# A hybrid decoder layer on one core: moving operands of TensorE laid out as two runs, even columns and odd columns

## The chip, the cores and the metric

The kernel runs on one core of one Trainium2 chip. The metric is the device time of one execution in microseconds: 2041.44 us is the median of three runs before the change (2040.09 to 2043.89). Engines are named as in the profile: PE (TensorE, with PEld for its weight loads), DVE (VectorE), ACT (ScalarE), POOL (GpSimd) and SP (SyncE, which issues the DMAs).

## The reference

One layer for 256 tokens of 2048 features, all in fp32: two SwiGLU blocks with 5632 hidden features around a token mixer, each behind an RMSNorm that a condition vector scales and shifts, and a last RMSNorm.

```python
def swiglu(h, wg, wu, wd):
    return (jax.nn.silu(h @ wg) * (h @ wu)) @ wd
...
    cond = jax.nn.silu(c)
    for l in range(DEPTH):
        mod = cond @ ada_w[l] + ada_b[l]
        sh1, sc1, gt1, sh2, sc2, gt2, sh3, sc3, gt3 = jnp.split(mod, N_MOD, axis=-1)
        h = ada_in(x, norm_g[l, 0], sh1, sc1)
        x = x + MACARON_W * gt1[:, None, :] * swiglu(h, ffn_w_gate[l, 0], ffn_w_up[l, 0], ffn_w_down[l, 0])
        h = ada_in(x, norm_g[l, 1], sh2, sc2)
        x = x + gt2[:, None, :] * hybrid_mixer(h, w_in[l], w_out[l], fox_f_bias[l], fox_out_norm[l],
                                               gdn_conv[l], gdn_A_log[l], gdn_dt_bias[l], gdn_out_norm[l])
        h = ada_in(x, norm_g[l, 2], sh3, sc3)
        x = x + MACARON_W * gt3[:, None, :] * swiglu(h, ffn_w_gate[l, 1], ffn_w_up[l, 1], ffn_w_down[l, 1])
    return rmsnorm(x, final_norm).astype(x.dtype)
```

`ada_in` is `rmsnorm(x, g) * (1 + scale) + shift`. The mixer projects `h` once, runs eight heads of forgetting attention (fox) and eight heads of a gated delta rule (gdn) side by side, and projects their outputs back with `w_out`.

## The kernel before

The activations stand with features on the partitions: a tile of 128 features by 256 tokens. All weights are 5392 tiles of 128x128, stored in the order in which the kernel uses them, eight to a block of 512 KB. `Stream.next` hands out the next tile. For a new block it starts the DMA into `wraw` (line 96), casts the block on ACT to a rounded fp32 format, `whi` (line 98), and subtracts on DVE to get the rest, `wlo` (line 110). Activations are split in the same way into a high part HI and a low part LO. A product is then made of three single-pass matmuls: high by high, high by low and low by high. Between blocks, at a pace set by the table `RATE`, `ada_col` fetches and reduces a row of the conditioning matrix (`mod`, line 230).

TensorE holds a weight tile and lets the activation pass as the moving operand, 256 columns of HI, 256 of LO, or 512 of both in one matmul:

- `hs` holds the normed input of a stage, 16 feature tiles `k` of LO, HI and a pad of 64 columns, of which two hold the split shift in the third norm (`Early`). Readers are `three` (first SwiGLU's first 28 hidden tiles, three matmuls of 256 columns, lines 518 to 520, outputs `pgu`), `mm_h` (the other gate and up tiles, one matmul of 512 columns and one of 256, lines 432 and 433, outputs `pg` and `pu`), `Early.products` (lines 376 to 378: the first three tiles of the second SwiGLU, with the two shift columns) and the mixer's `project` (lines 706 to 708, outputs `pp`).
- `hid` tiles hold the gated hidden features, `oh` tiles the heads' outputs, each as [HI, LO] of 256 columns. `mm` reads them (lines 436 and 437, outputs `pd` for the down projections and `po` for the output projection).
- In `project_rows` (lines 719 to 721, outputs `pv`) the roles change: a slice of `hs` is held, and four weight tiles of a block pass as 512 moving columns.

These operands are written by `modulate_one` and `Early.y` (`hs`), `split` (`hid`) and `out_split` (`oh`): ACT writes HI, then DVE writes LO.

The program's order is that of the code, with small reorderings by the scheduling layer; the mixer's heads are generators advanced by a clock that counts matmuls (`tick`, `start`, `finish`). The stages are: start and first SwiGLU up to about 770 us, the mixer to about 1290 us, with the output projection as its last 100 us, then the second SwiGLU and the last norm.

Of the kernel before, what the change touches and what calls it, by code (L numbers as in the profile page):

```python
# [28 lines left out]
WB = 8  # L29
# [13 lines left out]
HS = 2 * 256 + 64  # L43
# [26 lines left out]
N_COL = _n  # L70


class Stream:
# [27 lines left out]
    def next(self, mat, k, n, width=1):  # L101
# [13 lines left out]
        for d in range(width):  # L115
            self.order.append((mat, k, n + d))
        o = (i % WB) * P
        return self.h[:, o : o + width * P], self.l[:, o : o + width * P]
# [3 lines left out]
def layer_kernel(ctx: ExitStack, tc: tile.TileContext, xrow, c, adaw, cols, cst, w, out, order, dbg=None):  # L122
# [191 lines left out]
    hs = hsf[:, : KD * HS].rearrange("p (k i) -> p k i", k=KD)  # L314
    LO, HI, HIS, ALL = slice(0, T), slice(T, 2 * T), slice(T, 2 * T + 2), slice(0, 2 * T)

    def modulate_one(j, g1, sh, r):

        t = pt("ht")
        V.scalar_tensor_tensor(t, x[:, j], g1, r, ALU.mult, ALU.mult)  # L320
        if j % 2:
            A.activation(t, t, AF.Identity, bias=sh)
            A.copy(hs[:, j, HI], t)  # L323
            return V.tensor_tensor(hs[:, j, LO], t, hs[:, j, HI].bitcast(F32), ALU.subtract)
        else:
            with tc.issue_after(W.cast) if W.first else nullcontext():
                A.activation(hs[:, j, HI], t, AF.Identity, bias=sh)
            return V.scalar_tensor_tensor(hs[:, j, LO], t, sh, hs[:, j, HI].bitcast(F32), ALU.add, ALU.subtract)
# [8 lines left out]
    def modulate(which, m_sh, m_sc):  # L337
# [4 lines left out]
            j, g1[:, j : j + 1], mod[:, m_sh * KD + j : m_sh * KD + j + 1], r)  # L342

    class Early:
# [6 lines left out]
        def y(self, j):  # L351
# [3 lines left out]
            if j == 0:  # L355
                sh = mod[:, self.m_sh * KD : (self.m_sh + 1) * KD]
                A.copy(hs[:, :, 2 * T], sh)
                V.tensor_sub(hs[:, :, 2 * T + 1], sh, hs[:, :, 2 * T].bitcast(F32))
            g = gains(self.which, self.m_sc, j, 1)
            A.activation(hs[:, j, HI], x[:, j], AF.Copy, scale=g)  # L360
            V.scalar_tensor_tensor(hs[:, j, LO], x[:, j], g, hs[:, j, HI].bitcast(F32), ALU.mult, ALU.subtract)
# [13 lines left out]
        def products(self, ps, wt, k):  # L375
            PE.matmul(ps[:, : T + 2], wt[0], hs[:, k, HIS], start=(k == 0), stop=False)
            PE.matmul(ps[:, :T], wt[0], hs[:, k, LO], start=False, stop=False)
            PE.matmul(ps[:, : T + 2], wt[1], hs[:, k, HIS], start=False, stop=(k == KD - 1))
# [52 lines left out]
    def mm_h(ps, wt, k):  # L431
        PE.matmul(ps, wt[0], hs[:, k, ALL], start=(k == 0), stop=False)  # L432
        PE.matmul(ps[:, T:], wt[1], hs[:, k, HI], start=False, stop=(k == KD - 1))  # L433
# [908 lines left out]
```

## Time and profile before

| | |
|---|---|
| median of the runs | 2041.44 us (2040.09, 2041.44, 2043.89) |
| span of the profiled execution | 2038.5 us, granted TensorE clock 0.993 on average; the page gives no other time of this execution |
| PE, PEld | 98% and 89% busy |
| DVE, ACT, POOL | 77%, 50% and 3% busy |
| HBM read | 512.89 MB, 254 GB/s over the span |

The span runs from the first to the last instruction of one execution; a timed run also has what lies around it. [...]

### The profile page before, as it was taken

The page shows a single profiled execution, that of the slowest core. Times are in us where ns is not written, and L with a number is a line of the kernel's source. Part 1 is how long each engine was busy: PE and PEld are TensorE (multiplying, and loading weights), DVE is VectorE, ACT ScalarE, POOL GpSimd, SP SyncE. Part 2 cuts the span into 40 slices and gives each one's busy share as a digit, 9 for nine tenths or more (in the row PEclk, how much of TensorE's full clock was granted, in tenths as well). Part 3 has the DMA queues.
Part 4 walks back from the last instruction along what each step waited for, and adds up shares of the span by engine and source line. Part 5 has one row for each costly group of instructions (what it writes and reads, how often), then busy time and mean ns, then how long its engine had stood idle before and what let it go on. Part 6 is the DMA issues. An engine that isn't in the chain of part 4 may idle for free.

```text
span 2038.5 us, 33631 instructions
## 1 busy us (share of the span) xinstructions
PE 1998.6 (98%) x13058; PEld 1818.5 (89%) x13059; DVE 1566.0 (77%) x2424; ACT 1021.5 (50%) x1607; POOL 64.7 (3%) x60
## 2 busy tenths in 40 slices
PE   8999999999999999999999999999999999999997
PEld 6999999888888888889989988988888888888886
DVE  6898978889888998779878889976666555555555
ACT  6544544333444446666655655654444344444442
POOL 0000000000000120000000002000000000000012
PEclk9999999999999999999999999999999999999998
DMA  9999867999889885676666668667776655555553
GB/s 338 350 327 327 288 212 262 372 344 368 334 338 331 336 306 187 232 243 236 219 242 221 222 229 304 234 223 241 252 231 218 193 188 189 193 187 191 192 187 113
DMA packets 129489, 519.56 MB, mean 255 GB/s; under 512 B 18217, under 2 KB 21545, under 8 KB 111153
## 3 DMA queue, kind: packets, MB, share of 16 engines
q1 hardware_dynamic: 129330, 517.42, 72.1%
q8 instruction: 102, 1.67, 0.3%
q14 instruction: 57, 0.47, 0.1%
HBM read 512.89 MB, written 4.47 MB: 254 GB/s over the span
## 4 chain that ended last, share of the span: by engine, by line
PE 86%; DVE 6%; ACT 2%; DMA 2%; issue 2%; SPq 0%; DVEq 0%; ACTq 0%
PE pd L436 15%; PE pu L432 10%; PE pg L432 10%; PE pd L437 8%; PE pu L433 5%; PE pg L433 5%; PE pgu L520 5%; PE pgu L518 5%; PE pgu L519 5%; PE pp L706 3%; PE pp L708 3%; PE pp L707 3%; DVE wlo L110 2%; DMA wraw<-in_w_dram 2%; PE po L436 2%
## 5 line engine op out<-in xcount | busy, mean ns | idle before, releaser
L110 DVE TENSOR_TENSOR wlo<-wraw,whi 128x1024 fp32r<-128x1024 f32 x674 | 822.5, 1228 | 307.2 <-ACT whi L98 304.3
L98 ACT CAST whi<-wraw 128x1024 fp32r<-128x1024 f32 x674 | 702.0, 1049 | 630.2 <-issue 153.4
L436 PE MATMUL pd<-hid,whi 128*128 128x512 f32 x1408 | 488.5, 390 | 0.0
L437 PE MATMUL pd<-hid,wlo 128*128 128x256 f32 x1408 | 397.3, 282 | 1.0 <-DVE wlo L110 0.8
L230 DVE CUSTOM_DVE_ANT_0 adat<-adat,cs,colt 128x2048 f32<-128x2048 f32 x140 | 329.3, 2352 | 35.9 <-DMA adat<-in_ada_dram 35.7
L432 PE MATMUL pg<-hs,whi 128*128 128x512 f32 x912 | 318.9, 390 | 0.5 <-DVE shc L384 0.4
L432 PE MATMUL pu<-hs,whi 128*128 128x512 f32 x912 | 318.7, 390 | 0.0
L436 PEld LDWEIGHTS pd<-hid,whi 128*128 128x128 f32 x1408 | 264.1, 188 | 55.0
L437 PEld LDWEIGHTS pd<-hid,wlo 128*128 128x128 f32 x1408 | 266.1, 189 | 3.0 <-DVE wlo L110 2.7
L433 PE MATMUL pg<-hs,wlo 128*128 128x256 f32 x912 | 257.2, 282 | 0.0
L433 PE MATMUL pu<-hs,wlo 128*128 128x256 f32 x912 | 257.1, 282 | 0.0
L518 PE MATMUL pgu<-hs,whi 128*128 128x256 f32 x896 | 249.0, 281 | 6.8 <-ACT hs L323 5.7
L520 PE MATMUL pgu<-hs,wlo 128*128 128x256 f32 x896 | 248.0, 281 | 1.9 <-DVE wlo L110 1.8
L519 PE MATMUL pgu<-hs,whi 128*128 128x256 f32 x896 | 249.8, 281 | 0.0
L432 PEld LDWEIGHTS pg<-hs,whi 128*128 128x128 f32 x912 | 171.1, 188 | 36.7 <-ACT shc L383 0.5
L432 PEld LDWEIGHTS pu<-hs,whi 128*128 128x128 f32 x912 | 171.1, 188 | 35.7
L706 PE MATMUL pp<-hs,whi 128*128 128x256 f32 x656 | 189.7, 290 | 2.4 <-ACT whi L98 1.2
L708 PE MATMUL pp<-hs,wlo 128*128 128x256 f32 x656 | 186.2, 285 | 0.3 <-DVE wlo L110 0.3
L707 PE MATMUL pp<-hs,whi 128*128 128x256 f32 x656 | 185.7, 283 | 0.0
L518 PEld LDWEIGHTS pgu<-hs,whi 128*128 128x128 f32 x896 | 168.7, 189 | 7.7 <-ACT hs L323 6.1
L433 PEld LDWEIGHTS pu<-hs,wlo 128*128 128x128 f32 x912 | 172.3, 189 | 0.2
L433 PEld LDWEIGHTS pg<-hs,wlo 128*128 128x128 f32 x912 | 172.4, 189 | 0.0
(334 smaller groups left out, 2572.0 us busy)
## 6 DMA issues: line engine op xcount, KB each, us to landing
wraw<-in_w_dram SPq DMA_DIRECT2D x674, 512.0 KB, 4.4
adat<-in_ada_dram SPq DMA_DIRECT2D x140, 1024.0 KB, 7.1
xr<-in_xr_dram SPq DMA_DIRECT2D x4, 512.0 KB, 6.3
adaf<-in_ada_dram SPq DMA_DIRECT2D x4, 512.0 KB, 8.7
adaf<-in_ada_dram SPq DMA_DIRECT2D x2, 1024.0 KB, 12.5
xd<-x SPq DMA_DIRECT2D x4, 512.0 KB, 8.3
rw<-rowd SPq DMA_DIRECT2D x16, 128.0 KB, 6.7
x<-xd SPq DMA_DIRECT2D x4, 512.0 KB, 8.8
```

Source lines behind the costliest of these rows:

```text
L98: self.cast = self.nc.scalar.copy(self.h, r).ins
L110: nc.vector.tensor_tensor(self.l, r, self.h.bitcast(F32), ALU.subtract)
L230: V.tensor_tensor_reduce(t, t, cs, 1.0, L("adab", q, 1), ALU.mult, ALU.add, mod[:, q : q + 1])
L432: PE.matmul(ps, wt[0], hs[:, k, ALL], start=(k == 0), stop=False)
L433: PE.matmul(ps[:, T:], wt[1], hs[:, k, HI], start=False, stop=(k == KD - 1))
L436: PE.matmul(ps, wt[0], act.rearrange("p a t -> p (a t)"), start=first, stop=False)
L437: PE.matmul(ps[:, :T], wt[1], act[:, 0], start=False, stop=last)
L518: PE.matmul(o, wh, hs[:, k, HI], start=first and s == 0, stop=False, skip_group_check=skip)
L519: PE.matmul(o, wh, hs[:, k, LO], start=False, stop=False, skip_group_check=skip)
L520: PE.matmul(o, wl, hs[:, k, HI], start=False, stop=last, skip_group_check=skip)
L706: PE.matmul(pp[i][:, :T], wh, hs[:, k, HI], start=(k == 0), stop=False)
L708: PE.matmul(pp[i][:, :T], wl, hs[:, k, HI], start=False, stop=(k == KD - 1))
```

## The change

The moving operands named above, except those of `project`, are stored as two runs. Column 2b lies at place b of the first run and column 2b+1 at place b of the second. TensorE then reads first place 0 of both runs, then place 1 of both, and so on, so that the columns arrive in their old order: the access pattern's innermost step is from run to run, and the matmuls' outputs are unchanged. In `hs` a run is 128 columns and 16 of pad (576 bytes from run to run), the two shift columns take one place in the pad of each HI run. In `hid` and `oh` the runs are 128 columns (512 bytes apart). For the row projections the columns of four weight tiles are packed so by the host, as runs of 256 (1024 bytes apart). ACT and DVE write HI and LO through the same pattern. In the mixer's norm `hs` is written plainly (`weave=False`), because `project_rows` holds slices of it; `plain` is that view.

```diff
...
 HIDX = 3
 MORE = True
 
-HS = 2 * 256 + 64
+HA = 128 + 16
+HS = 4 * HA
 PAD = {"hs": 16, "w": 56, "hid": 16, "more": 56}
 
 BACK = (4, 6, 9)
...
 N_COL = _n
 
 
+def woven(ap):
+
+    return ap.rearrange("p (a b) -> p b a", a=2)
+
+
+def pairs(ap):
+
+    return ap.rearrange("p (b a) -> p b a", a=2)
+
+
 class Stream:
 
 
...
                 self.owed -= 1.0
                 self.side()
         for d in range(width):
-            self.order.append((mat, k, n + d))
+            self.order.append((mat, k, n, width, d))
         o = (i % WB) * P
-        return self.h[:, o : o + width * P], self.l[:, o : o + width * P]
+        h, l = self.h[:, o : o + width * P], self.l[:, o : o + width * P]
+        return (h, l) if width == 1 else (woven(h), woven(l))
 
 
 @with_exitstack
...
 
 
     hsf = keep.tile([P, KD * HS + PAD["w"]], F32R, name="hs")
-    hs = hsf[:, : KD * HS].rearrange("p (k i) -> p k i", k=KD)
-    LO, HI, HIS, ALL = slice(0, T), slice(T, 2 * T), slice(T, 2 * T + 2), slice(0, 2 * T)
-
-    def modulate_one(j, g1, sh, r):
+    hs = hsf[:, : KD * HS].rearrange("p (k q a b) -> p k q a b", k=KD, q=2, a=2)
+    LO, HI = 0, 1
+
+    plain = hsf[:, : KD * HS].rearrange("p (k i) -> p k i", k=KD)[:, :, : 2 * T].rearrange("p k (q t) -> p k q t", q=2)
+
+    def part(k, q, extra=0):
+        return hs[:, k, q, :, : P + extra].rearrange("p a b -> p b a")
+
+    def modulate_one(j, g1, sh, r, weave=True):
 
         t = pt("ht")
+        hl, hh, tt = (part(j, LO), part(j, HI), pairs(t)) if weave else (plain[:, j, LO], plain[:, j, HI], t)
         V.scalar_tensor_tensor(t, x[:, j], g1, r, ALU.mult, ALU.mult)
         if j % 2:
             A.activation(t, t, AF.Identity, bias=sh)
-            A.copy(hs[:, j, HI], t)
-            return V.tensor_tensor(hs[:, j, LO], t, hs[:, j, HI].bitcast(F32), ALU.subtract)
+            A.copy(hh, tt)
+            return V.tensor_tensor(hl, tt, hh.bitcast(F32), ALU.subtract)
         else:
             with tc.issue_after(W.cast) if W.first else nullcontext():
-                A.activation(hs[:, j, HI], t, AF.Identity, bias=sh)
-            return V.scalar_tensor_tensor(hs[:, j, LO], t, sh, hs[:, j, HI].bitcast(F32), ALU.add, ALU.subtract)
+                A.activation(hh, tt, AF.Identity, bias=sh)
+            return V.scalar_tensor_tensor(hl, tt, sh, hh.bitcast(F32), ALU.add, ALU.subtract)
 
     def gains(which, m_sc, j, n):
 
...
         g1 = gains(which, m_sc, 0, KD)
         r = norm_row(norm_sums())
         hq["next"], hq["one"] = 0, lambda j: modulate_one(
-            j, g1[:, j : j + 1], mod[:, m_sh * KD + j : m_sh * KD + j + 1], r)
+            j, g1[:, j : j + 1], mod[:, m_sh * KD + j : m_sh * KD + j + 1], r, False)
 
     class Early:
 
...
             ada_need(self.m_sh, KD - 1)
             if j == 0:
                 sh = mod[:, self.m_sh * KD : (self.m_sh + 1) * KD]
-                A.copy(hs[:, :, 2 * T], sh)
-                V.tensor_sub(hs[:, :, 2 * T + 1], sh, hs[:, :, 2 * T].bitcast(F32))
+                A.copy(hs[:, :, HI, 0, P], sh)
+                V.tensor_sub(hs[:, :, HI, 1, P], sh, hs[:, :, HI, 0, P].bitcast(F32))
             g = gains(self.which, self.m_sc, j, 1)
-            A.activation(hs[:, j, HI], x[:, j], AF.Copy, scale=g)
-            V.scalar_tensor_tensor(hs[:, j, LO], x[:, j], g, hs[:, j, HI].bitcast(F32), ALU.mult, ALU.subtract)
+            A.activation(part(j, HI), pairs(x[:, j]), AF.Copy, scale=g)
+            V.scalar_tensor_tensor(part(j, LO), pairs(x[:, j]), g, part(j, HI).bitcast(F32), ALU.mult, ALU.subtract)
 
         def step(self, k):
 
...
                 h_upto(min(k, k - 4 + max(0, k - 10)))
 
         def products(self, ps, wt, k):
-            PE.matmul(ps[:, : T + 2], wt[0], hs[:, k, HIS], start=(k == 0), stop=False)
-            PE.matmul(ps[:, :T], wt[0], hs[:, k, LO], start=False, stop=False)
-            PE.matmul(ps[:, : T + 2], wt[1], hs[:, k, HIS], start=False, stop=(k == KD - 1))
+            PE.matmul(ps[:, : T + 2], wt[0], part(k, HI, 1), start=(k == 0), stop=False)
+            PE.matmul(ps[:, :T], wt[0], part(k, LO), start=False, stop=False)
+            PE.matmul(ps[:, : T + 2], wt[1], part(k, HI, 1), start=False, stop=(k == KD - 1))
 
         def scaled(self, dst, ps):
 
...
         chains[kind].append((h, chain))
 
     def mm_h(ps, wt, k):
-        PE.matmul(ps, wt[0], hs[:, k, ALL], start=(k == 0), stop=False)
-        PE.matmul(ps[:, T:], wt[1], hs[:, k, HI], start=False, stop=(k == KD - 1))
+        both = hs[:, k, :, :, :P].rearrange("p q a b -> p q b a")
+        PE.matmul(ps, wt[0], both, start=(k == 0), stop=False)
+        PE.matmul(ps[:, T:], wt[1], part(k, HI), start=False, stop=(k == KD - 1))
 
     def mm(ps, wt, act, first, last):
-        PE.matmul(ps, wt[0], act.rearrange("p a t -> p (a t)"), start=first, stop=False)
-        PE.matmul(ps[:, :T], wt[1], act[:, 0], start=False, stop=last)
+        PE.matmul(ps, wt[0], act.rearrange("p q (a b) -> p q b a", a=2), start=first, stop=False)
+        PE.matmul(ps[:, :T], wt[1], woven(act[:, 0]), start=False, stop=last)
 
     def merge(dst, ps, scale=None):
 
...
             V.scalar_tensor_tensor(dst, ps[:, :T], scale, t, ALU.mult, ALU.add)
 
     def split(dst, src):
-        A.copy(dst[:, 0], src)
-        V.tensor_sub(dst[:, 1], src, dst[:, 0].bitcast(F32))
+        A.copy(woven(dst[:, 0]), pairs(src))
+        V.tensor_sub(woven(dst[:, 1]), pairs(src), woven(dst[:, 0]).bitcast(F32))
 
     def residual(ps, j, m_gt, half):
         ada_need(m_gt, j)
...
             wh, wl = W.next(("gu"[s], 0), k, f)
             first, last = k == k0, k == k1 - 1
             skip = s == 1
-            PE.matmul(o, wh, hs[:, k, HI], start=first and s == 0, stop=False, skip_group_check=skip)
-            PE.matmul(o, wh, hs[:, k, LO], start=False, stop=False, skip_group_check=skip)
-            PE.matmul(o, wl, hs[:, k, HI], start=False, stop=last, skip_group_check=skip)
+            PE.matmul(o, wh, part(k, HI), start=first and s == 0, stop=False, skip_group_check=skip)
+            PE.matmul(o, wh, part(k, LO), start=False, stop=False, skip_group_check=skip)
+            PE.matmul(o, wl, part(k, HI), start=False, stop=last, skip_group_check=skip)
 
         turn = [0]
 
...
                 m, n = items[i]
                 h_need(k)
                 wh, wl = W.next(m, k, n)
-                PE.matmul(pp[i][:, :T], wh, hs[:, k, HI], start=(k == 0), stop=False)
-                PE.matmul(pp[i][:, :T], wh, hs[:, k, LO], start=False, stop=False)
-                PE.matmul(pp[i][:, :T], wl, hs[:, k, HI], start=False, stop=(k == KD - 1))
+                PE.matmul(pp[i][:, :T], wh, plain[:, k, HI], start=(k == 0), stop=False)
+                PE.matmul(pp[i][:, :T], wh, plain[:, k, LO], start=False, stop=False)
+                PE.matmul(pp[i][:, :T], wl, plain[:, k, HI], start=False, stop=(k == KD - 1))
                 tick(TILE_US)
             return [p_[:, :T] for p_ in pp]
 
...
             for k in range(KD):
                 wh, wl = W.next(mat, k, 4 * grp, 4)
                 for t in range(2):
-                    sl = slice(t * P, (t + 1) * P)
-                    PE.matmul(pv[t], hs[:, k, HI][:, sl], wh, start=(k == 0), stop=False)
-                    PE.matmul(pv[t], hs[:, k, HI][:, sl], wl, start=False, stop=False)
-                    PE.matmul(pv[t], hs[:, k, LO][:, sl], wh, start=False, stop=(k == KD - 1))
+                    hh, hl = (plain[:, k, q, t * P : (t + 1) * P] for q in (HI, LO))
+                    PE.matmul(pv[t], hh, wh, start=(k == 0), stop=False)
+                    PE.matmul(pv[t], hh, wl, start=False, stop=False)
+                    PE.matmul(pv[t], hl, wh, start=False, stop=(k == KD - 1))
                     tick(2 * TILE_US)
             return pv
 
...
         def out_split(i, ps, g):
 
             o = oh_[i] = otile("oh")
-            A.activation(o[:, 0], ps, AF.Copy, scale=g)
-            V.scalar_tensor_tensor(o[:, 1], ps, g, o[:, 0].bitcast(F32), ALU.mult, ALU.subtract)
+            A.activation(woven(o[:, 0]), pairs(ps), AF.Copy, scale=g)
+            V.scalar_tensor_tensor(woven(o[:, 1]), pairs(ps), g, woven(o[:, 0]).bitcast(F32), ALU.mult, ALU.subtract)
 
 
         def fox(h, qk, vt):
...
         mats[("u", s)] = v["ffn_w_up"][0, s]
         mats[("d", s)] = v["ffn_w_down"][0, s]
     w = np.empty((N_TILES // WB, P, WB, P), np.float32)
-    for i, (m, k, n) in enumerate(order):
-        w[i // WB, :, i % WB] = mats[m][k * P : (k + 1) * P, n * P : (n + 1) * P]
+    for i, (m, k, n, width, d) in enumerate(order):
+        cols = n * P + np.arange(width * P)
+        if width > 1:
+            cols = cols.reshape(-1, 2).T.ravel()
+        w[i // WB, :, i % WB] = mats[m][k * P : (k + 1) * P, cols[d * P : (d + 1) * P]]
     return w.reshape(N_TILES // WB, P, WB * P)
 
 
```

On every engine the instructions stand in the same order as before, with the same counts and sizes, except for one pair. `Early.y(0)` copies the shift to `hs` on ACT and makes its low part on DVE. These are ACT's rows around the copy before, in the middle of the mixer (`whi` is a weight block, `qv`, `cv` and `Tm` belong to a gated head, `pp` is a projection):

```order
L1073 ACTIVATE oh<-pft,colt 128x256
L858 ACT_TABLE_LOAD
L858 ACTIVATE qv<-cv 128x256
L855 ACTIVATE cv<-pp,colt 128x256
L957 COPY Tm_8267<-pu_11077 64x2x64
L98 CAST whi<-wraw 128x1024
L357 CAST hs<-mod 128x16
L98 CAST whi<-wraw 128x1024
L1173 ACTIVATE x<-pp 128x256
```

And these are ACT's rows around it now, at the mixer's last projection (line 1192 is the former 1173, `orw` is a gated head's output):

```order
L1132 ACTIVATE j_13240,fss<-pfo 128x128
L109 CAST whi<-wraw 128x1024
L1092 ACTIVATE oh<-pft,colt 128x128x2
L1192 ACTIVATE x<-pp 128x256
L109 CAST whi<-wraw 128x1024
L375 CAST hs<-mod 128x16
L1068 COPY orw<-po 64x256
L1069 COPY orw<-po 64x256
```

The copy (line 357, now 375) has moved behind the last reading of a plain projection's result; before, its columns lay outside the 512 that the projections read, now they lie inside. DVE's step has moved with it. The row of `oh` also shows the new form of a write, 128x128x2 for 128x256.

## The prediction, on record before the result

> **What bounds the kernel now.** I read the page's busy shares first, then the chain that ended last.
>
> ```profile
> PE 1998.6 (98%) x13058; PEld 1818.5 (89%) x13059; DVE 1566.0 (77%) x2424; ACT 1021.5 (50%) x1607; POOL 64.7 (3%) x60
> PE 86%; DVE 6%; ACT 2%; DMA 2%; issue 2%; SPq 0%; DVEq 0%; ACTq 0%
> ```
>
> TensorE is busy 98% of the span and holds 86% of the chain. A busy PE is not a PE at its peak, so the next question is how far apart its matmuls start. The table of stages answers that where nothing waits: count the PE instructions in 100 us.
>
> ```profile
> core 0: us, PE busy (x) PEld busy (x) DVE busy (x) ACT busy (x) POOL busy (x), PEclk, DMA share, GB/s
> 140.00:240.00 100.00, 100.00 (x859) 100.00 (x858) 91.89 (x121) 46.42 (x60) 0.00 (x0) 1.00 0.88 313
> 240.00:340.00 100.00, 100.00 (x860) 100.00 (x859) 76.59 (x114) 48.84 (x72) 0.00 (x0) 1.00 0.68 228
> 420.00:520.00 100.00, 99.01 (x565) 86.36 (x564) 88.69 (x100) 36.66 (x38) 0.00 (x0) 1.00 0.96 359
> 1420.00:1520.00 100.00, 100.00 (x579) 88.67 (x578) 66.89 (x83) 49.31 (x74) 0.00 (x0) 1.00 0.73 239
> 1720.00:1820.00 100.00, 100.00 (x578) 88.66 (x578) 57.18 (x73) 48.17 (x72) 0.00 (x0) 1.00 0.58 190
> 400.00:700.00 300.00, 299.01 (x1718) 263.70 (x1718) 262.62 (x301) 129.94 (x172) 1.20 (x1) 1.00 0.92 344
> ```
>
> The first two rows are the first SwiGLU's gate and up: all matmuls have 256 moving columns, and 100/859.5 gives one every 116.4 ns. Rows four and five are the later stages, where a 512-column and a 256-column matmul alternate: 200/578.5 gives 345.7 ns a pair. The granted clock is 1.00, so nothing is throttled. The timeline splits the pair (start, duration, engine, line).
>
> ```profile
> 1720.64 0.39 PE L432 MATMUL pu<-hs,whi 128*128 128x512 f32 x1
> 1720.87 0.28 PE L433 MATMUL pu<-hs,wlo 128*128 128x256 f32 x1
> 1720.99 0.39 PE L432 MATMUL pu<-hs,whi 128*128 128x512 f32 x1
> ```
>
> The 512 columns hold the engine 230 ns, the 256 columns 116 to 120 ns. The trace has two other kinds of matmul to hold this against: 2-byte ones, and full fp32 ones whose records read 128 columns.
>
> ```profile
> 20.03 1.46 PE L173 MATMUL zp<-zw 128*128 128x512 bf16 x6
> L173 PE MATMUL zp<-zw x16: 379/634/634, 1.2 to 21.1; 128*128 128x512 bf16 x16
> 890.39 0.61 PE L953 MATMUL pkq<-qv,kk 128*128 128x128 f32 x4
> 890.84 0.38 PE L870 MATMUL pk<-colt,kk 128*128 128x128 f32 x2
> L953 PEld LDWEIGHTS pkq<-qv,kk x32: 188/192/192, 890.3 to 1171.2; 128*128 128x128 f32 x32
> ```
>
> Six bf16 matmuls of 512 columns last 1.46 us together and one lasts 379 ns (the minimum: the fast ones), so they start (1460 - 379)/5 = 216 ns apart. The fp32 records start 450/4 = 112 ns apart, with weight loads of 192 ns beside them. At (390 - 282)/256 = 0.42 ns a column (the mean durations of the pair, in the rows below), 112 ns is the time of 256 columns plus 4 ns: these records read 4-byte columns, but at half the rate.
>
> So the operands that this change touches pay something. A pair would take 216 + 108 = 324 ns at the bf16 spacing and takes 345.7, and a 256-column matmul would take 108 and takes 116.4. That excess, 6 to 7%, is all that a new order of reading can win.
>
> **The change, part by part.** Groups by line give the counts of the touched matmuls; L433 and L437 have the counts of L432 and L436, L519 and L520 that of L518, L720 and L721 that of L719.
>
> ```profile
> L436 PE MATMUL pd<-hid,whi 128*128 128x512 f32 x1408 | 488.5, 390 | 0.0
> L437 PE MATMUL pd<-hid,wlo 128*128 128x256 f32 x1408 | 397.3, 282 | 1.0 <-DVE wlo L110 0.8
> L432 PE MATMUL pg<-hs,whi 128*128 128x512 f32 x912 | 318.9, 390 | 0.5 <-DVE shc L384 0.4
> L432 PE MATMUL pu<-hs,whi 128*128 128x512 f32 x912 | 318.7, 390 | 0.0
> L518 PE MATMUL pgu<-hs,whi 128*128 128x256 f32 x896 | 249.0, 281 | 6.8 <-ACT hs L323 5.7
> L436 PE MATMUL po<-oh,whi 128*128 128x512 f32 x256 | 89.8, 392 | 0.0
> L719 PE MATMUL pv<-whi,hs 128*128 128x512 f32 x128 | 52.5, 412 | 2.6 <-DVE cv L857 1.6 <-ACT whi L98 0.9
> L376 PE MATMUL pg<-hs,whi 128*128 128x258 f32 x48 | 13.7, 286 | 0.0
> 1043.11 0.40 PE L720 MATMUL pv<-wlo,hs 128*128 128x512 f32 x1
> 1043.81 0.40 PE L720 MATMUL pv<-wlo,hs 128*128 128x512 f32 x1
> ```
>
> That is 1408 + 912 + 912 + 256 = 3488 pairs, 3 x 896 = 2688 single matmuls of 256 columns, 384 of the row projections (three in 0.70 us, 233 ns each), and 6 x 48 = 288 early ones. The projections on L706 to L708 keep the old layout. No matmul is added.
>
> What does reading in turn do to the excess? No operand of TensorE in this trace is read so, and the cost is bounded from both sides. Best case: all of it goes, 3488 x 21.7 = 76, 2688 x 8.4 = 23, 384 x 17 = 7, 288 x 8 = 2, together 108 us. Worst case: each column costs what it costs in the fp32 rows, worked out as a rival below, +1510 us. Between them I reason as follows. The fp32 records have the same loads beside them and read 4-byte columns; their excess is 4 ns where the touched ones' is 8.4. What differs is the rate at which the moving read walks through memory. Two runs read in turn are each walked at half the rate, as in those rows, so I take their 112 ns for 256 columns and 216 + 4 = 220 for 512. A pair then takes 332: 3488 x 13.7 = 47.8, 2688 x 4.4 = 11.8, 384 x 13 = 5.0, 288 x 4 = 1.2; 66 us. That the rate causes the excess is an inference; no row shows it.
>
> [...]
>
> Not all 66 us reach the end. In 400 to 700 us the DMA engines are busy 0.92, and 0.96 where PE did only 565 instructions; 859 pairs there would save 11.8 us, and I count half as lost to late weights (6 us). In 140 to 240 us DVE is at 92%; of 1200 matmuls' 5.3 us there I count 2 as lost.
>
> Writing the runs: each splitting step on ACT and DVE now writes alternately to two places.
>
> ```profile
> L450 ACT CAST hid<-tu 128x256 fp32r<-128x256 f32 x88 | 35.4, 403 | 68.3 <-DVE tu L467 66.4 <-DVE tu L493 1.9
> L451 DVE TENSOR_TENSOR hid<-tu,hid x88: 416/420/427, 226.7 to 1905.7; 128x256 fp32r<-128x256 f32 x88
> L361 DVE SCALAR_TENSOR_TENSOR hs<-x,g,hs x16: 474/958/970, 1220.6 to 1292.1; 128x256 fp32r<-128x256 f32 x16
> ```
>
> There are 88 hidden tiles, 16 + 16 of hs and 16 of oh, 136 pairs of steps. No row shows such a write. If it costs nothing, nothing changes; if it doubles (L361 shows that a step can go from 474 to 958 ns here), DVE gets 136 x 0.42 = 57 us and ACT 55. A gain is excluded: the count of elements stays. I take 1 us, the plain steps being the nearest rows. DVE's 77% and ACT's 50% cover it; in the first 700 us DVE's cover is thin.
>
> The two copies of the shifts (L357, L358) move behind the last plain projection, since their column now lies inside what it reads.
>
> ```profile
> L357 ACT CAST hs<-mod x1: 218/218/218, 1006.1 to 1006.1; 128x16 fp32r<-128x16 f32 x1
> L708 PE MATMUL pp<-hs,wlo x656: 274/280/415, 779.9 to 1192.9; 128*128 128x256 f32 x164
> L360 ACT ACTIVATE hs<-x,g x16: 492/494/496, 1219.9 to 1291.6; 128x256 fp32r<-128x256 f32 x16
> ```
>
> The projections end at 1193 us and the first step behind the copies starts at 1219.9: 27 us of the output projection hide 0.4 us of copies. Behind them on ACT and DVE stand a weight cast and the gated heads' last steps; no DMA is moved. Without that cover it would cost 0.4 us.
>
> Sum: 66 - 6 - 2 - 1 = 57 us off the profiled span of 2038.5, 1981.5. The page gives no other time of that execution; the median of 2041.4 is 2.9 above the span, which I add: 1984.4 us.
>
> **The rivals.** *Half-rate read (slower).* If a column that lies elsewhere than the one before it needs a step of its own, the touched matmuls read at the fp32 rows' rate: 224 ns for 256 columns, 440 for 512. Pairs: 3488 x (664 - 345.7) = 1110; singles 2688 x 108 = 290; rows 384 x 207 = 79; early 288 x 108 = 31; +1510, 3552 us. It decides at every column or not at all. For it: every touched operand is now read so that no column follows its neighbour in memory. Against it: nothing in the trace is read that way. [...] Chance 0.17.
>
> *The two runs clash (slower).* Runs of hid and oh lie 512 bytes apart, those of hs 576. If equal spacing makes one run wait for the other, the excess of 21.7 ns doubles on the 1408 + 256 pairs of L436 and L437: +36, 2077 us, with no gain elsewhere. Chance 0.08.
>
> *The writes decide (slower).* PE gains nothing and the writes double: 44 of the hidden tiles and 16 of hs fall in the first 700 us, 60 x 0.42 = 25 us on a DVE at about 88%; half on the path gives +13, 2054 us. Chance 0.09.
>
> *Nothing happens.* The excess is a fixed cost of a 4-byte load: 2041 us. For it: it is nearly as large for 256 columns as, per matmul, for 512 (8 and 14 ns). Chance 0.08.
>
> **How the numbers follow.** Forecast 0.58, the rivals 0.17 + 0.08 + 0.09 slower and 0.08 unchanged. About 0.2% is what a measurement of this kernel can tell from no change: faster 0.58, same 0.08, slower 0.34. The likeliest case alone reaches from 1940 (108 us less some 10 lost, with the 2.9) to 2025 (a quarter of the 66). The range goes up over the two mild slower cases to 2105, not quite twice the clash's price of 36 above 2041; outside stay the half-rate read and 0.03 beyond the ends.
>
> **What would show it.** Right: over 580 PE instructions in 100 us of the later stages (332 ns a pair would be 602), 890 in the first SwiGLU, L706 unchanged, L451 near 420 ns, DVE busier than 92% at 140 to 240 us. Half rate: 300 instructions in 100 us. Clash: the pairs of pd slower than those of pg and pu. I am wrong about the cause if 512 and 256 columns lose equal amounts.

## The result and the profile after

The changed kernel takes 1983.44 us (median of 4 runs, 1978.01 to 1985.42) beside 2042.66 us of the kernel before on the same chip (4 runs, 2040.09 to 2045.78): a ratio of 0.971, 95% interval 0.969 to 0.972. The profiled execution took 1983.29 us, with a span of 1981.5.

The page of the kernel after, engines' busy time and the chain that ended last:

```profile
PE 1919.3 (97%) x13059; PEld 1783.2 (90%) x13059; DVE 1582.2 (80%) x2424; ACT 1045.7 (53%) x1607; POOL 64.2 (3%) x60
PE 66%; DVE 14%; DMA 10%; issue 6%; ACT 4%; SPq 0%; DVEq 0%; ACTq 0%
```

TensorE is busy for 79.3 us less (1998.6 before), and the span is 57.0 us shorter: so TensorE is idle for 62.2 us where it was idle for 39.9. Its share of the chain fell from 86% to 66%, and DVE and DMA took over most of what it gave up (from 6% to 14% and from 2% to 10%). The stages of the kernel after show the same two things side by side:

```profile
core 0: us, PE busy (x) PEld busy (x) DVE busy (x) ACT busy (x) POOL busy (x), PEclk, DMA share, GB/s
140.00:240.00 100.00, 98.46 (x882) 98.27 (x881) 93.89 (x122) 48.18 (x62) 0.00 (x0) 1.00 0.87 317
240.00:340.00 100.00, 99.22 (x887) 98.83 (x886) 80.67 (x120) 52.92 (x74) 0.00 (x0) 1.00 0.68 235
400.00:500.00 100.00, 97.91 (x590) 88.52 (x589) 93.06 (x106) 37.98 (x38) 0.00 (x0) 1.00 0.99 377
1780.00:1880.00 100.00, 100.00 (x613) 91.99 (x612) 62.59 (x79) 51.49 (x72) 2.78 (x2) 1.00 0.59 201
```

In the last row nothing waits: 613 instructions where the kernel before has 579 in the same 100 us. In the row of 400 to 500 us the DMA engines are full (0.99), and only 590 fit. How far apart the starts lie in a pair is seen in the timeline of the kernel after (start, duration, engine, line):

```profile
1649.74 0.38 PE L451 MATMUL pu<-hs,whi 128*128 128x512 f32 x1
1649.96 0.27 PE L452 MATMUL pu<-hs,wlo 128*128 128x256 f32 x1
...
1650.39 0.38 PE L451 MATMUL pu<-hs,whi 128*128 128x512 f32 x1
1650.61 0.27 PE L452 MATMUL pu<-hs,wlo 128*128 128x256 f32 x1
1650.72 0.38 PE L451 MATMUL pg<-hs,whi 128*128 128x512 f32 x1
```

L451 lasts 380 ns and the next matmul starts 220 ns after it, so what a matmul costs is read from the starts and not from its length. Three pairs in 0.98 us. Over all pairs of 1780 to 1880 us the mean distance is 327.5 ns; taken in the same way it was 346.7 before (the 345.7 of the prediction came from counting in a window, which is an instruction coarse). Two groups by line (busy us, mean ns of one), and the rows of two lines:

```profile
L455 PE MATMUL pd<-hid,whi 128*128 128x512 f32 x1408 | 462.1, 382 | 0.8 <-DVE hid L470 0.8
L456 PE MATMUL pd<-hid,wlo 128*128 128x256 f32 x1408 | 384.6, 273 | 3.0 <-DVE wlo L121 3.0
L469 ACT CAST hid<-tu x88: 648/659/686, 224.0 to 1853.6; 128x256 fp32r<-128x256 f32 x88
L470 DVE TENSOR_TENSOR hid<-tu,hid x88: 608/623/642, 224.7 to 1854.8; 128x256 fp32r<-128x256 f32 x88
```

L455 and L456 are the former L436 and L437; each matmul lasts 8 to 9 ns less. The projections (L725, the former L706) read plainly as before, and their matmuls still start 117 ns apart. The last two rows (minimum, median, maximum) are the steps that write `hid`: 403 ns became 659 on ACT, 420 became 623 on DVE. For the waits, one row of before and then two of after (engine, line, what it waited for: us in total, times, longest):

```profile
ACT whi L98 <- DMA wraw<-in_w_dram: 150.7, 79, 5.9
```

```profile
ACT whi L109 <- DMA wraw<-in_w_dram: 195.0, 124, 5.8
DVE adat L242 <- DMA adat<-in_ada_dram: 52.2, 30, 3.8
```

The cast of the weights waits 44 us longer for its data. The forecast number came true; whether its parts did, and its cause, is for the experiments to show.

### The profile page after: what moved, and what is told of

It reads as the page before. It is cut to its first block, busy times and chain, and to the rows that moved or that the text cites. A ratio compares the mean times of both kernels' runs of the same rounds, so it can differ in the third digit from the quotient of the medians.

```text
span 1981.5 us, 33632 instructions
## 1 busy us (share of the span) xinstructions
PE 1919.3 (97%) x13059; PEld 1783.2 (90%) x13059; DVE 1582.2 (80%) x2424; ACT 1045.7 (53%) x1607; POOL 64.2 (3%) x60
## 4 chain that ended last, share of the span: by engine, by line
PE 66%; DVE 14%; DMA 10%; issue 6%; ACT 4%; SPq 0%; DVEq 0%; ACTq 0%
PE pd L455 12%; PE pg L451 9%; PE pu L451 9%; PE pd L456 6%; DVE wlo L121 6%; DMA adat<-in_ada_dram 5%; PE pu L452 5%; PE pg L452 5%; DMA wraw<-in_w_dram 4%; PE pgu L539 3%; PE pgu L538 3%; PE pgu L537 3%; PE pp L725 2%; PE pp L727 2%; PE pp L726 2%
## 5 line engine op out<-in xcount | busy, mean ns | idle before, releaser
L455 PE MATMUL pd<-hid,whi 128*128 128x512 f32 x1408 | 462.1, 382 | 0.8 <-DVE hid L470 0.8
L456 PE MATMUL pd<-hid,wlo 128*128 128x256 f32 x1408 | 384.6, 273 | 3.0 <-DVE wlo L121 3.0
L451 PE MATMUL pg<-hs,whi 128*128 128x512 f32 x912 | 303.8, 384 | 3.9 <-ACT whi L109 2.8
L451 PE MATMUL pu<-hs,whi 128*128 128x512 f32 x912 | 302.6, 382 | 0.0
L455 PEld LDWEIGHTS pd<-hid,whi 128*128 128x128 f32 x1408 | 266.0, 189 | 38.0 <-DVE hid L470 1.4
L456 PEld LDWEIGHTS pd<-hid,wlo 128*128 128x128 f32 x1408 | 270.5, 192 | 5.9 <-DVE wlo L121 5.7
L537 PE MATMUL pgu<-hs,whi 128*128 128x256 f32 x896 | 245.9, 277 | 8.4 <-ACT hs L341 6.7
L452 PE MATMUL pu<-hs,wlo 128*128 128x256 f32 x912 | 249.9, 274 | 0.5 <-DVE wlo L121 0.3
L452 PE MATMUL pg<-hs,wlo 128*128 128x256 f32 x912 | 249.6, 274 | 0.0
L538 PE MATMUL pgu<-hs,whi 128*128 128x256 f32 x896 | 245.9, 276 | 0.1
L451 PEld LDWEIGHTS pg<-hs,whi 128*128 128x128 f32 x912 | 173.2, 190 | 28.6 <-issue 3.0
L725 PE MATMUL pp<-hs,whi 128*128 128x256 f32 x656 | 189.9, 291 | 4.2 <-ACT whi L109 1.4
L451 PEld LDWEIGHTS pu<-hs,whi 128*128 128x128 f32 x912 | 172.4, 189 | 23.6
```

The lines of the kernel that those rows point to most:

```text
L451: PE.matmul(ps, wt[0], both, start=(k == 0), stop=False)
L452: PE.matmul(ps[:, T:], wt[1], part(k, HI), start=False, stop=(k == KD - 1))
L455: PE.matmul(ps, wt[0], act.rearrange("p q (a b) -> p q b a", a=2), start=first, stop=False)
L456: PE.matmul(ps[:, :T], wt[1], woven(act[:, 0]), start=False, stop=last)
L537: PE.matmul(o, wh, part(k, HI), start=first and s == 0, stop=False, skip_group_check=skip)
L538: PE.matmul(o, wh, part(k, LO), start=False, stop=False, skip_group_check=skip)
```

## The experiments

All kernels were run against the kernel before on the same chip: the first four together (before 2040.71 us), the next four together (2042.23), the last two together (2040.72), each the median of 9 runs.

**What a plain read loses, and to what.** A kernel of its own runs 48 matmuls of each kind, one kind after the other, with nothing else on TensorE.

```diff
+ go(lambda i: PE.matmul(o(i, 256, 8), w(i, 8), run(8), ...))    # plain, 8-column loads
+ go(lambda i: PE.matmul(o(i), w(i), turn(8, 128), ...))         # two runs in turn
+ go(lambda i: PE.matmul(o(i), w(i), step(8, 2), ...))           # every other column
```

> Not the layer: 48 matmuls in a row of each of some twenty kinds, and eight of each kind of write, all on data of the right types; nothing of the reference is computed. What counts is the distance between starts. Both theories give 110 to 112 ns for 256 columns read from two runs in turn with 128-column weight loads, and 116 to 119 for one plain run. Theory A (the plain read walks twice as fast as the weight load beside it and meets it): with loads of 8 columns the plain run drops to 108 to 110, and the plain run's time depends on its offset to the weights (0, 16, 32, 64, 128, 192 bytes) by 2 ns or more; in four runs in turn 110 to 112. Theory B (the plain read alone loses time, whatever is loaded beside it): with loads of 8 columns the plain run stays at 115 to 119 and in turn at 109 to 112; the offset makes no difference over 1 ns. Rival rule (a column in another line than the one before costs a step): columns 16 and 32 bytes apart take 200 ns or more, and two runs with two columns of each in turn take less than with one of each. Writes of 256 elements: straight 400 to 420 ns on ACT and DVE; in turn 620 to 660; run by run with a source step of two 400 to 450 if the scattered writing is what costs, 620 or more if the step in the source costs as much.

The timeline of this kernel (start of the block, its length, line; a block's distance from start to start is the time to the next block's start, by 48):

```profile
39.30 5.76 PE L65 MATMUL b<-buf 128*8 128x256 f32 x48
44.90 5.76 PE L66 MATMUL b<-buf 128*128 128x256 f32 x48
50.50 5.92 PE L67 MATMUL b<-buf 128*128 128x256 f32 x48
...
78.78 5.52 PE L72 MATMUL b<-buf 128*128 128x256 f32 x48
84.14 5.52 PE L73 MATMUL b<-buf 128*128 128x256 f32 x48
89.50 5.52 PE L74 MATMUL b<-buf 128*128 128x256 f32 x48
...
100.22 5.40 PE L76 MATMUL b<-buf 128*8 128x256 f32 x48
105.46 7.04 PE L77 MATMUL b<-buf 128*128 128x256 f32 x48
112.33 8.48 PE L78 MATMUL b<-buf 128*128 128x256 f32 x48
120.64 11.16 PE L79 MATMUL b<-buf 128*128 128x256 f32 x48
131.61 11.39 PE L80 MATMUL b<-buf 128*128 128x256 f32 x48
142.80 10.65 PE L81 MATMUL b<-buf 128*128 128x256 f32 x48
...
164.49 11.29 PE L83 MATMUL b<-buf 128*8 128x512 f32 x48
175.61 10.52 PE L84 MATMUL b<-buf 128*128 128x512 f32 x48
185.97 10.52 PE L85 MATMUL b<-buf 128*8 128x512 f32 x48
```

A plain read with loads of 8 columns (L65) takes 5.60 us for 48, 116.7 ns each, and with loads of 128 columns (L66, the same weight tile each time) 116.7 as well. So at this start in memory the excess doesn't come from the weight load. Two runs in turn with loads of 128 columns take 111.7 ns, whether they lie 512 bytes (L72) or 576 (L73) apart; with loads of 8 columns they take 109.2 (L76), where the plain read took 116.7. 512 columns go from 231.7 ns read plainly (L83, loads of 8 columns) to 215.8 in turn (L84, loads of 128 columns; L85, with loads of 8, lasts as long). Every other column of one run (L79), which is a step of 8 bytes, takes 228.5 ns. Four runs (L77) take 143, two columns of each run in turn (L78) 173: it is not "the more runs the better".

Neither theory came out whole. Theory A is right that the start in memory matters (the plain read takes 114 to 120 ns over the starts tried here), but fails with the small loads and with the four runs, for which it had 110 to 112 ns. Theory B has the small loads right, but allowed the start 1 ns. The rival rule has the steps of 16 and 32 bytes right (233 ns in L80, 218 in L81), but fails with L78, which at 173 ns takes more than L72 with 111.7 and not less.

The same kernel times the writes, eight steps of each kind (minimum, median, maximum):

```profile
L102 ACT CAST d<-x x8: 399/404/406, 14.8 to 17.8; 128x256 fp32r<-128x256 f32 x8
L103 DVE TENSOR_TENSOR d<-x,d x8: 424/426/426, 18.3 to 21.5; 128x256 fp32r<-128x256 f32 x8
L104 ACT CAST d<-x x8: 637/638/642, 22.0 to 26.7; 128x256 fp32r<-128x256 f32 x8
L105 DVE TENSOR_TENSOR d<-x,d x8: 609/614/619, 27.4 to 31.9; 128x256 fp32r<-128x256 f32 x8
L106 ACT CAST d<-x x8: 418/420/423, 32.6 to 35.8; 128x256 fp32r<-128x256 f32 x8
L107 DVE TENSOR_TENSOR d<-x,d x8: 425/426/426, 36.2 to 39.4; 128x256 fp32r<-128x256 f32 x8
```

Straight, in turn, and one run after the other with the source read at every other element: only the alternating step is dear, and the third way, which puts the same numbers in the same places, costs 16 ns or nothing. On ACT the alternating write alone is new; DVE's step also reads HI alternately, and these rows don't part the two.

**How far apart the columns of a stream lie.** An account of the author's, which no row shows by itself, would fit the spacings of 111.7 (L72), 116.7 (L66) and 228.5 ns (L79): suppose that the even and the odd columns are two streams, and that the distance in memory from a column to the next of its stream sets the cost. Two runs in turn give each stream a run of its own, its columns 4 bytes apart; in a plain read they lie 8 bytes apart; at a step of 8 bytes, 16. (Counted as in the expectation below, that is four, two and one in 16 bytes.) A second kernel of the same kind tries that.

```diff
+ go(lambda i: PE.matmul(o(i), w(i), turns(8, 512, 2), ...))     # in turn, columns 8 bytes apart
+ go(lambda i: PE.matmul(o(i), w(i), turns(8, 1024, 4), ...))    # in turn, 16 bytes apart
+ go(lambda i: PE.matmul(o(i), w(i), fours(8), ...))             # four columns of each run in turn
```

> Not the layer: rows of 48 matmuls as in the first such kernel, nothing of the reference is computed. Theory C, formed from the first one: even and odd columns are fetched as two streams, and each stream loses time when it gets fewer than four columns from 16 bytes of memory (four: 109 to 112 ns for 256 columns, two: 113 to 120, one: 218 to 233). By C two runs in turn whose columns lie 8 bytes apart take 113 to 120 as a plain run does, 16 bytes apart 218 to 233, and four columns of each run in turn 113 to 125. Theory D (what counts is how far each column lies from the one before it, two places being cheap): two runs with columns 8 bytes apart stay at 110 to 112, four of each in turn take over 140. On the offset: if it counts from the memory's own grid, plain runs at offset 0 and 192 bytes keep 120 and 113 ns when the weights move by 64 bytes and with loads of 8 columns; if it counts from the weights, moving them by 64 bytes gives 113 and 119.

```profile
38.66 5.52 PE L81 MATMUL b<-buf 128*128 128x256 f32 x48
44.02 5.82 PE L82 MATMUL b<-buf 128*128 128x256 f32 x48
49.67 11.18 PE L83 MATMUL b<-buf 128*128 128x256 f32 x48
60.65 10.76 PE L84 MATMUL b<-buf 128*128 128x256 f32 x48
71.21 5.53 PE L85 MATMUL b<-buf 128*128 128x192 f32 x48
...
76.58 6.27 PE L86 MATMUL b<-buf 128*128 128x256 f32 x48
82.69 5.86 PE L87 MATMUL b<-buf 128*128 128x256 f32 x48
```

In turn with the columns side by side 111.7 ns (L81), 8 bytes apart 117.7 (L82), 16 bytes apart 228.8 (L83): the second costs about what the plain read costs (116.7), the third as much as the plain step of 8 bytes (228.5). That is what the account foretells. Four columns of each run in turn (L86) take 127.3 ns, a little above the upper end of 125 for it, and the 143 and 173 ns of the first kernel, where a stream changes between two places and comes back, have no number from this account. Theory D fails at both of its places (117.7 and 127.3 where it had 110 to 112 and over 140).

One row of this kernel bears on the 111.7 ns themselves: 192 columns in turn (L85) start 111.8 ns apart, as 256 do. With loads of 8 columns 256 of them took 109.2. Both speak for the load of 128 columns, and not the read, as what sets 111.7. The blocks on the start in memory fit neither account that was given for them: at start 0 a plain read takes 116.9 ns with small loads and 117.7 with the weights moved (119.9 in the first kernel), at 192 bytes 113.5 and 120.2, and the same block at 192 bytes took 114.0 in the first kernel and 117.7 in this one.

**The two halves of the change.** First the writes alone: the kernel before, with the splitting steps writing in turn and TensorE reading straight.

```diff
-        A.copy(dst[:, 0], src)
-        V.tensor_sub(dst[:, 1], src, dst[:, 0].bitcast(F32))
+        A.copy(woven(dst[:, 0]), pairs(src))
+        V.tensor_sub(woven(dst[:, 1]), pairs(src), woven(dst[:, 0]).bitcast(F32))
```

> The kernel before, in which hid, oh, the first norm's hs and the third norm's hs are written in turn into two runs, but read straight; the columns of the products are therefore in a wrong order. The touched matmuls keep 345 to 346 ns a pair and 116 for a single one. ACT's and DVE's 136 writes each take 0.2 to 0.25 us longer. If these writes are what ate the difference between the saved TensorE time and the saved span (about 84 and 57 us), the kernel comes out 8 to 25 us slower than before (2050 to 2067 us). If the loss comes from late weights instead, it is within 6 us of before.

It takes 2048.64 us, 7.9 us more (ratio 1.0041, 1.0025 to 1.0056, so 5 to 11 us). That lies between the two ranges. The steps that write `hid` take 671 ns on ACT and 633 on DVE (medians). Where the 7 us of the span come from can be counted, since TensorE does the same instructions in the same order: an instruction that starts at 780 us in the kernel before starts 0.7 us later here, at 1190 us 0.9, at 1320 us 3.5 and at 1330 us 7.1, and the distance then stays near 7. So about a third is lost in the output projection, and half at one point behind the third norm. There the second SwiGLU's first regular pair waits for a step of DVE (`shc`), 2.0 us longer than before (before, then with these writes):

```profile
PE pg L432 <- DVE shc L384: 0.4, 1, 0.4
```

```profile
PE pg L441 <- DVE shc L393: 2.4, 1, 2.4
```

Then the reads alone: the kernel after, writing straight.

```diff
-        A.copy(woven(dst[:, 0]), pairs(src))
-        V.tensor_sub(woven(dst[:, 1]), pairs(src), woven(dst[:, 0]).bitcast(F32))
+        A.copy(dst[:, 0], src)
+        V.tensor_sub(dst[:, 1], src, dst[:, 0].bitcast(F32))
```

> The kernel after with straight writes: the same bytes are written in the plain order and read in turn, so the columns of the products come in a wrong order. Pairs at 327 to 328 ns as after, writes at 400 to 425 ns as before. If the longer writes ate the missing 27 us, 1958 to 1972 us; if late weights did, 1978 to 1984 us, as after.

1972.41 us, 68.3 less than before (ratio 0.9661, 0.9648 to 0.9675), just above the first range. The reads alone bring 68, the change as a whole 59, and the writes cost the difference of 9, about what they cost alone. Counted as above, the change as made falls behind these straight writes by 2.6 us up to 700 us, 5.2 up to 1287, 8.6 up to 1300 and 10.4 up to 1600.

**The same layout, written run by run.** The whole computation, with the loops of each write exchanged: first the even columns, then the odd ones, from a source read at every other element.

```diff
-        A.copy(woven(dst[:, 0]), pairs(src))
+        A.copy(runs(dst[:, 0]), columns(src))
...
+def runs(ap):      # ap.rearrange("p (a b) -> p a b", a=2)
+def columns(ap):   # ap.rearrange("p (b a) -> p a b", a=2)
```

> The kernel after, complete, with the two loops of each write exchanged: it writes one whole run and then the other, and reads its source with a step of two. If a step of two in the source is free, this equals the kernel with straight writes: writes of 400 to 430 ns and 1958 to 1975 us. If the step costs as much as the scattered write did, 1980 to 1986 us.

```profile
L482 ACT CAST hid<-tu x88: 415/434/519, 222.7 to 1840.4; 128x256 fp32r<-128x256 f32 x88
L483 DVE TENSOR_TENSOR hid<-tu,hid x88: 408/421/508, 223.3 to 1841.7; 128x256 fp32r<-128x256 f32 x88
```

1975.67 us, 65.0 less than before (ratio 0.9673, 0.9656 to 0.9691). This is just above the range for a free step in the source; the steps take 434 and 421 ns. This version beats both kernels; against the change as made it gains 6 to 9 us, judged by the distances from before.

**Where the rest of the gain goes.** In both the kernel before and the run-by-run one, the conditioning rows from the third part on are left out: 112 transfers of 1 MB and as many reductions on DVE of 2.35 us.

```diff
+        if m >= 2:
+            V.memset(mod[:, q : q + 1], 0.1)
+            return
```

> The kernel before without the conditioning rows of m >= 2: 112 DMAs of 1 MB and their reductions on DVE (2.35 us each) are left out, mod is a constant there. TensorE's work is the same. If TensorE alone bounds the kernel, it gains no more than its present waits, 2010 to 2035 us.

> The kernel with run-by-run writes, with the same rows left out as in the one before it. About 84 us of TensorE time are saved by reading in turn, of which 65 reached the end with the rows in. If late weights and a busy DVE took the other 19, the distance between these two kernels is 75 to 85 us; if something else did, 62 to 70 us.

2030.04 us (ratio 0.994, 0.9926 to 0.9955) and 1950.80 us (0.9555, 0.9541 to 0.9568). With these rows gone the new reads bring 79.2 us; with them in, 65.0, and 67.7 in the second run of that kernel, told below. So 12 to 14 us of the gain are lost to what these rows occupy, give or take some 4 us by the intervals (an estimate). The waits of the run-by-run kernel, with the rows and then without:

```profile
ACT whi L119 <- DMA wraw<-in_w_dram: 187.3, 110, 5.9
```

```profile
ACT whi L119 <- DMA wraw<-in_w_dram: 65.9, 41, 5.9
```

In the kernel before, that wait falls too, from 150.7 to 49.2 us, and only 12 us of time are gained with it: most of that wait cost nothing here. Transfers and reductions went together here, so these runs don't say how much of it is DMA and how much is DVE.

**Would the projections gain too?** The run-by-run kernel, in which the mixer's 41 projections also read two runs in turn (the two halves of the plain row). Their results then leave PSUM in another order, which 24 added copies on ACT put right.

```diff
-                PE.matmul(pp[i][:, :T], wh, plain[:, k, HI], ...)
+                PE.matmul(pp[i][:, :T], wh, woven(plain[:, k, HI]), ...)
...
+            cr = pt("cr")
+            A.copy(runs(cr), columns(ps))
```

> The kernel with run-by-run writes, complete, in which the mixer's 41 projections read in turn too: the two halves of the plain 256 tokens are the two runs, so the outputs' columns come as token 0, 128, 1, 129 and are put right where they leave PSUM. 1968 matmuls at 111 to 112 ns instead of 117 would save 10 us; ACT gets 24 more copies of 0.4 us. If TensorE bounds the mixer, 1964 to 1971 us; if its chains of small steps and late weights do, within 3 us of the kernel with run-by-run writes (1975.7).

A miss: 1989.38 us (ratio 0.9739, 0.9723 to 0.9754). By the distances from before this gains 52.9 us, 12 to 15 less than run by run. The projections' matmuls start 112 ns apart, as foretold, but 100 us of the mixer show what that is worth, first run by run and then with the projections:

```profile
780.00:880.00 100.00, 94.21 (x612) 83.69 (x611) 83.14 (x200) 70.00 (x137) 0.42 (x2) 1.00 0.69 234
```

```profile
780.00:880.00 100.00, 83.95 (x527) 74.35 (x526) 75.66 (x169) 72.14 (x133) 0.42 (x2) 0.93 0.59 204
```

TensorE does 527 instructions where it did 612. It is idle for 16.1 us where it was for 5.8, and 11.7 of them until a weight block is cast on ACT or split on DVE (3.0 before): both engines do these steps between those of the heads' chains, which the copies made longer. The granted clock is also lower in this stretch, 0.93 beside 1.00. That the copies are behind all of it is argued, not shown. To take the copies out of that, only the queries and keys of the fox heads, which need no added step, read in turn:

```diff
+                way = woven if m in ("qf", "kf") else (lambda ap: ap)
-                    A.activation(qk[:, i], pp[i], AF.Copy, ...)
+                    A.activation(runs(qk[:, i]), columns(pp[i]), AF.Copy, ...)
```

> This is the run-by-run kernel, with one more part of TensorE's moving reads turned to the new order: of the mixer's projections only the 16 of the queries and keys of the future side are read in turn, and nothing is added on any other engine. 16 projections are 768 matmuls of 256 columns, from 116.7 to 111.7 ns each, so 3.8 us of TensorE's time in the mixer. Theory 'TensorE bounds the mixer': 1 to 5 us faster than run_by_run_again on the same chip. Theory 'the chains of the heads bound the mixer' (which the run with all projections spoke for, where an added copy lengthened these chains by 14 us): within 2 us of run_by_run_again.

> The run-by-run kernel once more, as the yardstick beside the queries and keys in turn on the same chip: 1973 to 1978 us, 0.966 to 0.969 of the kernel before. Every theory expects that; outside it, the order of the runs or the chip sets some of the differences of a few us told here.

1971.59 us (ratio 0.9665, 0.9650 to 0.9679) beside 1973.01 (0.9665, 0.9652 to 0.9678). The difference of 1.4 us lies inside both accounts and inside the intervals: this run decides nothing, beyond that there is little left to win here.

## Why the prediction was right, and where it was not

The forecast of 1984.4 us lies 1 us from the median. That it came so close is luck: the gross gain and the loss were each 23 us too small, and the two errors cancel. A small term was off as well: the 2.9 us between span and time are 1.8 in the profiled execution of the changed kernel (1983.29 and 1981.5).

**The gross gain was sized too small.** I let a pair go to 332 ns; it went to 327.5, near the 324 of the best case. 3488 pairs by 19.2 ns are 67.0 us where I had 47.8; 2688 single matmuls by 5.0 (the micro kernel's 116.7 and 111.7) 13.4 where I had 11.8; 384 row matmuls by 17 (233 to 216) 6.5 where I had 5.0; the early ones under 2. Together 89 us, not 66. The term that failed is the 4 ns for each matmul, taken from fp32 records of another kind: for 512 columns nothing is left above the 216 ns of bf16 (215.8), and for 256 most of the rest goes with the load (109.2 ns when it is small).

**The loss was sized too small.** 32 of these 89 us didn't reach the end, and I had 9. The writes, put at 1 us, cost 5 to 11: no row showed such a write, and I took the row of the plain step when the other bound stood at twice that; measured is 1.5 to 1.6 times. DVE's 77% and ACT's 50% were no cover, because most of the cost falls where TensorE waits for one chain of steps, and not where DVE is busiest. The supply, put at 8 us for two stages, costs 12 to 14. My 6 us for 400 to 700 us were about right: in 400 to 680 us the run-by-run kernel does 1683 instructions on TensorE with the conditioning rows and 1709 without, 26 x 164 ns = 4 us. (For 140 to 240 us I counted 1200 matmuls; the row has 859, which save 3.8 us by my 4.4 ns, not 5.3.) What I left out is that the supply is tight elsewhere too. The output projection's 256 pairs should save 4.9 us; from the first of them to the last it takes 94.1 us before and 94.9 after (92.7 and 88.5 with the conditioning rows left out), and it now waits 4.7 us for low weights (1.9 before). These rows end, before their shapes, with the first and the last start, before and then after:

```profile
L436 PE MATMUL po<-oh,whi x256: 388/390/580, 1193.0 to 1287.1; 128*128 128x512 f32 x128
```

```profile
L455 PE MATMUL po<-oh,whi x256: 380/382/567, 1166.7 to 1261.6; 128*128 128x512 f32 x128
```

```profile
PE po L456 <- DVE wlo L121: 4.7, 6, 1.9
```

Some 10 us remain: they are missing even without conditioning rows and slow writes (89 against 79.2). By the traces of the two kernels without those rows, most lie in two places. At the start the first 32 conditioning rows were left in, and the 2688 single matmuls of `three` are run in 7.9 us less where 13.4 were due (first to last start 22.7 to 347.1 us with the old reads, 22.6 to 339.1 with the new). In 24 to 140 us TensorE does 905 instructions with the old reads and 902 with the new, with DVE busy for 107 of these 116 us, DMA at 0.92 and 0.90 and a granted clock of 0.99 and 0.96: nothing is gained there, and my sum has no loss before 140 us. In the mixer the row projections should save 6.5 us, and from its first projection's start to its last's it takes 407.3 us and then 404.0, 3.3 less.

**The cause was wrong.** I inferred that the plain read loses by its rate: it walks through memory twice as fast as the fp32 rows, with the same loads beside it. Two things speak against that. With loads of 8 columns instead of 128 the plain read takes the same 116.7 ns, and 7.5 more than two runs in turn with these loads. And four runs, each walked at a quarter of the rate, take 143 ns and not 111.7. So at the start tried the plain read loses its time whichever the load (116.7 ns with 8 columns and with 128), and reading in turn takes most of the loss away (109.2 and 111.7 ns). What I put in its place, two streams whose cost goes by the distance of their columns, fits 111.7, 116.7 and 117.7, 228.5 and 228.8 ns at distances of 4, 8 and 16 bytes, but it is an account of mine that no row shows by itself. Its finer cases (127.3, 143 and 173 ns), and the few ns by which the start in memory moves a plain read (113 to 120 ns), are open. My sign for a wrong cause, equal losses of 512 and 256 columns, could not serve: inside a pair the two lose 9 to 10 ns each, by themselves 16 (231.7 to 215.8) and 5.

**The rivals.** The half-rate read did not come: 613 instructions in 100 us, not 300. But its price was real, for another pattern: a step of 8 bytes costs 228.5 ns, where I had 224. No run had then shown what such a read costs, and the chance of 0.17 was an estimate. The clash of two runs did not come either: 512 and 576 bytes apart both give 111.7 ns, and the pairs of `pd` start 327.5 ns apart, as those of `pg` and `pu` do. *The writes decide* was right that longer writes reach the end, but not on its place and size: 8 us, not 13, 0.6 us of it in the first 700 us with the old reads and 2.6 with the new, and not instead of the gain but out of it. *Nothing happens* is off by 59 us; a cost of the load is left in the last 2.5 of the 111.7 ns.

**The signs.** 613 against the 602 named, 887 against 890 in the first SwiGLU, L706 unchanged, and DVE at 93.89% where I said over 92%: these held. DVE's split at 420 ns (623 measured) did not, and that miss is the one behind the writes' cost.

## What to carry to other kernels

An fp32r moving operand read straight through loses 4 to 8% here (116.7 ns beside 111.7 and 109.2 for 256 columns, 231.7 beside 215.8 for 512); if it lies as two runs, even columns and odd columns, the loss almost goes. Write such a layout run by run with a strided source, never by alternating writes (434 and 421 ns on ACT and DVE beside 659 and 623), and add no step to a chain that the matmuls wait for in order to get it: the longer writes cost 5 to 11 us here, most of it where TensorE waited for one chain of steps, with DVE 77% and ACT 50% busy on average before. When a TensorE that was 98% busy gets faster, look at the stages in which DMA or DVE stand above 90%: here a quarter (run by run) to over a third (the change as made) of the 89 us stayed there and in the new steps' cost.

## What the runs showed of the hardware that was not expected

- A moving read of 256 four-byte columns: 116.7 ns straight, 111.7 as two runs in turn, 228.5 at a step of 8 bytes (L79), 233 at 16 (L80), 218 at 32 (L81). From 8 to 32 bytes the cost doesn't grow.
- Matmuls of 256 and of 192 columns, both in turn and with loads of 128 columns, start 111.7 and 111.8 ns apart; with loads of 8 columns 256 take 109.2. A loss that looked like the read's was here in part the load's.
- The time of a straight read also moved with its start in memory and from kernel to kernel: at another start 5.92 us for 48 (L67) instead of 5.76 (L66), and 113 to 120 ns each over the starts tried, not reproducibly by the start alone (192 bytes: 114.0 in one kernel, 117.7 in the other). Two runs in turn gave 111.7 at each of three starts (0, 32 and 192 bytes).
- ACT and DVE write 256 elements alternately to two places in 638 and 614 ns, straight in 404 and 426; *reading* the source at every other element and writing run by run costs 16 ns or nothing (in the layer 31 and 1).
